# A hybrid decoder block: where the meta rows are loaded, how the first two tiles are normalized, and when the last 16 rows and V's second blocks are handled

## The chip, the cores and the metric

The kernel runs on one core of a Trainium2 chip. The metric is the device time of one execution in microseconds (us); several executions are timed, and one more is recorded by the hardware profiler. The engines are PE (TensorE, matrix products; PEld is its weight loads), DVE (VectorE), ACT (ScalarE), POOL (GpSimd) and SP (SyncE, which here only issues DMA transfers). ACTq and SPq are the instruction queues of ACT and SP where they issue transfers. Each engine takes its instructions in the order in which the program lists them.

## The reference

1,024 rows of `x` with 16 learned meta rows ahead of them (1,040 rows of 1,024 columns) are normalized, projected once into all branches, mixed by causal pooling and by attention with forget gates, merged and projected back.

```python
h = concat([meta, x])                               # 1040 x 1024
h = h * rsqrt(mean(h * h) + 1e-6) * norm_g
proj = h @ w_in                                     # u, z, q, k, v, z_attn, f, g_pool, g_attn
y_pool = (trailing_mean(u) - u) @ pool_w * pool_scale * silu(z_pool)
y_attn = forgetting_attention(q, k, v, log_sigmoid(f + b_forget)) * silu(z_attn)
merged = sigmoid(g_pool) * (y_pool @ w_up_pool) + sigmoid(g_attn) * (y_attn @ w_up_attn)
out = rmsnorm(x + merged @ w_out, final_norm_g)     # meta rows dropped
```

## The kernel before

Only the startup is touched, the first 60 us of some 743. It does three things.

**Normalizing.** The 1,040 rows are nine tiles `xts[0]` to `xts[8]`, eight of 128 rows and the last of 16. Tile 0 is filled by two transfers on SP's queue, 112 rows of `x` and the 16 meta rows (`norm_load`, L171). `norm_stat` (L182) squares a tile on ACT with a running sum (`ss`), which ACT reads out in an instruction of its own; `rstd_of` (L110) adds the epsilon on DVE (L113) and takes the power -0.5 on POOL (L114). `norm_scale` (L187) multiplies the tile in two halves of 512 columns on DVE by the row's `rstd` and by `gb`. `gb` holds `norm_g` in all 128 rows; two products on PE make it in PSUM from one row of ones and the loaded `norm_g` (L391), with `warm_up` products around them.

**Transposing.** `norm_t` (L192) transposes a scaled tile on PE into PSUM in two halves of four 128 x 128 blocks (`pt`, `pn`). ACT copies each half, rounded, to `hh` (L212), and DVE subtracts this from PSUM to get the rest, `hl` (L213). Only then is the PSUM buffer free. `pt` comes from a pool of two buffers, `pn` is a single one; tile 6 uses both `pt`, tile 7 `pn` and then the `pt` that tile 6's first half had, the 16-row tile the other `pt`.

**Projecting.** Weights are split in the same way into `whi` and `wlo` (L401, L406). For the first head pair, Q, K and V are computed for four pieces of the sequence (`todo`, twelve steps n = 0 to 11: q, k, v for 0:256, 256:512, 512:768, 768:1040). One piece is 24 products (L152): eight `hh,whi`, eight `hl,whi`, eight `hh,wlo`. Q's results are copied by ACT to `qa` and by DVE to `ql` (L241, L245), K's to `ka` (L263, L266), V's by ACT to `vt` (L270). `v_blocks` (L276) transposes two 128-row blocks of `vt` on PE, and ACT and DVE write `V` (L284, L285). The 16-row tile's transposes stand inside step n = 8, behind its eight `hh,whi` products.

The order of all this on every engine is the order of the code (a manual schedule), written in the loop over `todo`: behind step n it transposes a tile ahead, scales another, and now and then makes blocks of V.

Of the kernel before, what the change touches and what calls it, by code (L numbers as in the profile page):

```python
# [8 lines left out]
F32 = mybir.dt.float32  # L9
F32R = mybir.dt.float32r  # L10
AF = mybir.ActivationFunctionType
ALU = mybir.AluOpType
AX = mybir.AxisListType

D = 1024
NM = 16
# [4 lines left out]
EPS = 1e-6  # L21
# [22 lines left out]
def r32(ap):  # L44
    return ap.bitcast(F32)
# [7 lines left out]
def tile_hybrid_block(ctx, tc, x, meta, norm_g, w_in, b_forget, pool_w, pool_scale,  # L53
                      w_up_pool, w_up_attn, w_out, final_g, out):
    nc = tc.nc
# [14 lines left out]
    sm = ctx.enter_context(tc.tile_pool(name="sm", bufs=2))  # L70
# [4 lines left out]
    psG = G_.enter_context(tc.tile_pool(name="psG", bufs=1, space=PS))  # L75
# [4 lines left out]
    epsp = cst.tile([128, 1], F32, name="epsp")  # L80
# [29 lines left out]
    def rstd_of(ss):  # L110
        n = ss.shape[0]
        r = sm.tile([128, 1], F32, name="rstd", bufs=4)
        nc.vector.tensor_scalar(r[:n], ss, EPS, None, op0=ALU.add)  # L113
        nc.gpsimd.tensor_tensor(r[:n], r[:n], epsp[:n], op=ALU.pow)  # L114
        return r
# [45 lines left out]
    def run(g):  # L161
        for _ in g:
            pass
# [1 line left out]
    A = ExitStack()  # L165
    ap_ = A.enter_context(tc.tile_pool(name="ap", bufs=1))

    gb = psG.tile([128, 2, 512], F32, name="gb")
    junk = gp.tile([128, D], F32, name="junk", tag="g")

    def norm_load(i):  # L171
        c0 = i * 128
        n = min(128, L - c0)
        xt = ap_.tile([128, D], F32, name="xt", tag="s", bufs=6)
        if i == 0:
            nc.sync.dma_start(xt[NM:], x2[:128 - NM, :])
            nc.sync.dma_start(xt[:NM], meta)
        else:
            nc.sync.dma_start(xt[:n], x2[c0 - NM:c0 - NM + n, :])
        return xt  # L180

    def norm_stat(xt, n):  # L182
        ss = sm.tile([128, 1], F32, name="ss")
        nc.scalar.activation(junk[:n], xt[:n], AF.Square, scale=D ** -0.5, accum_out=ss[:n])
        return rstd_of(ss[:n])

    def norm_scale(xt, n, r):  # L187
        for j, (c0, c1) in enumerate(HALVES):
            nc.vector.scalar_tensor_tensor(xt[:n, c0:c1], xt[:n, c0:c1], r[:n], gb[:n, j],
                                           op0=ALU.mult, op1=ALU.mult)  # L190

    def norm_t(i0, xt, n):  # L192
        c0 = i0 * 128
        if n < 128:
            both = psT.tile([128, KO, n], F32, name="pt")
            for i in range(KO):
                nc.tensor.transpose(both[:, i, :], xt[:n, i * 128:(i + 1) * 128], ident[:n, :n])
            for j in range(2):
                h_ = hh4[j][:, :, c0:c0 + n]
                part = both[:, 4 * j:4 * j + 4]  # L200
                nc.scalar.activation(h_, part, AF.Copy)  # L201
                last = nc.vector.tensor_tensor(hl4[j][:, :, c0:c0 + n], part, r32(h_), op=ALU.subtract)
            return last
        for j in range(2):
            if (2 * i0 + j) % 3 == 2:
                pt = psG.tile([128, 4, 128], F32, name="pn")
            else:
                pt = psT.tile([128, 4, 128], F32, name="pt")
            for i in range(4):
                nc.tensor.transpose(pt[:, i, :n], xt[:n, (4 * j + i) * 128:(4 * j + i + 1) * 128], ident[:n, :n])  # L210
            h_ = hh4[j][:, :, c0:c0 + n]
            nc.scalar.activation(h_, pt[:, :, :n], AF.Copy)  # L212
            last = nc.vector.tensor_tensor(hl4[j][:, :, c0:c0 + n], pt[:, :, :n], r32(h_), op=ALU.subtract)  # L213
        return last
# [21 lines left out]
    def q_piece(p, w, t0, t1):  # L236
        c0, c1 = t0 - NM, t1 - NM
        ps = yield from g_proj(w, t0, t1)

        def hi(e, r):  # L240
            nc.scalar.activation(QA[p, e][r, c0:c1], ps[rows(e)[0]], AF.Copy, scale=0.125)  # L241

        def lo(e):
            a, _ = rows(e)
            nc.vector.scalar_tensor_tensor(QL[p, e][a, c0:c1], ps[a], 0.125, r32(QA[p, e][a, c0:c1]),  # L245
                                           op0=ALU.mult, op1=ALU.subtract)

        for group in EVAC[p > 0]:
            for e in group:
                hi(e, rows(e)[0])  # L250
                if not p:
                    hi(e, rows(e)[1])
            for e in group:
                lo(e)
                if p:
                    hi(e, rows(e)[1])

    def k_piece(p, w, t0, t1):
        ps = yield from g_proj(w, t0, t1)
        for group in EVAC[p > 0]:  # L260
            for e in group:
                a, o = rows(e)
                nc.scalar.activation(KA[p, e][a, t0:t1], ps[a], AF.Copy)  # L263
            for e in group:
                a, o = rows(e)
                nc.vector.tensor_tensor(KA[p, e][o, t0:t1], ps[a], r32(KA[p, e][a, t0:t1]), op=ALU.subtract)  # L266

    def v_piece(p, w, t0, t1):
        ps = yield from g_proj(w, t0, t1)
        nc.scalar.activation(VT[p][:, t0:t1], ps, AF.Copy)  # L270

    def v_alloc(p):
        for e in range(2):
            V[p, e] = ap_.tile([KB, NB, 2, 64], F32R, name="V", bufs=3)

    def v_blocks(p, b0, b1):  # L276
        pt = pj.tile([128, 4, 2, 64], F32, name="pj")
        for b in range(b0, b1):
            nc.tensor.transpose(pt[:, b - b0], VT[p][:, KS[b]:KS[b] + KB], ident)  # L279
            yield 109.0  # L280
        pv = pt[:, :b1 - b0]
        for e in range(2):
            vh = V[p, e][:, b0:b1, e, :]
            nc.scalar.activation(vh, pv[:, :, e, :], AF.Copy)  # L284
            nc.vector.tensor_tensor(V[p, e][:, b0:b1, 1 - e, :], pv[:, :, e, :], r32(vh), op=ALU.subtract)  # L285
# [91 lines left out]
    onesr = cst.tile([128, 128], F32R, name="onesr")  # L377
    nc.vector.memset(r32(onesr), 1.0)
    grow = ap_.tile([1, D], F32, name="grow", tag="t")
    nc.scalar.dma_start(grow, norm_g)  # L380
    nc.scalar.activation(junk[:1, :2], r32(onesr)[:1, :2], AF.Square)
    xts = {0: norm_load(0), 1: norm_load(1)}
    warm = psG.tile([128, 4, 128], F32, name="pn")

    def warm_up(n):
        for _ in range(n):
            nc.tensor.matmul(warm, onesr, onesr[:, None, :].to_broadcast([128, 4, 128]), start=True, stop=True)

    warm_up(WARM[0])
    for j, (c0, c1) in enumerate(HALVES):  # L390
        nc.tensor.matmul(gb[:, j], r32(onesr)[:1], grow[:, c0:c1], start=True, stop=True)  # L391
    warm_up(WARM[1])

    def load_raw(col, pool=None, tag="raw"):
# [4 lines left out]
    def split_hi(raw, pool, tag):  # L399
        hi = pool.tile([128, KO, 128], F32R, name="whi", tag=tag)  # L400
        nc.scalar.activation(hi, raw, AF.Copy)  # L401
        return hi

    def split_lo(raw, hi, pool, tag):
        lo = pool.tile([128, KO, 128], F32R, name="wlo", tag=tag)
        nc.gpsimd.tensor_tensor(lo, raw, r32(hi), op=ALU.subtract)  # L406
        return hi, lo
# [7 lines left out]
    def ntok(i):  # L415
        return min(128, L - 128 * i)

    alloc_k(0)
    for i in range(2):
        norm_scale(xts[i], 128, norm_stat(xts[i], 128))  # L420
    hq_ = split_hi(rq, wp, "wh")
    norm_t(0, xts[0], 128)
    wq = split_lo(rq, hq_, wp, "wl")
# [10 lines left out]
    for n, (kind, t0, t1) in enumerate(todo):  # L434
        if n + 4 < 9:
            xts[n + 4] = norm_load(n + 4)
        if kind == "q":
            run(q_piece(0, wq, max(NM, t0), t1))
        elif kind == "k":
            run(k_piece(0, wk, t0, t1))  # L440
        else:
            g = v_piece(0, wv, t0, t1)
            if n == 8:
                for _ in range(KO):
                    next(g)
                norm_t(8, xts[8], ntok(8))
            run(g)
        i = {0: 2, 1: 3, 3: 4, 4: 5, 6: 6, 7: 7}.get(n)
        if i is not None:
            norm_t(i, xts[i], ntok(i))  # L450
        if n == 0:
            hv_ = split_hi(rv, gp, "g")
            wv = split_lo(rv, hv_, gp, "g")
            VT[0] = gp.tile([128, L], F32, name="vt", tag="g")
            v_alloc(0)
        i = {1: 4, 2: 5, 4: 6, 5: 7, 6: 8}.get(n)
        if i is not None:
            norm_scale(xts[i], ntok(i), norm_stat(xts[i], ntok(i)))
        if n == 2:
            zero_q(0)  # L460
        if n == 4:
            wf = sm.tile([128, KO, H], F32, name="wf", bufs=1)
            nc.sync.dma_start(wf, w_in2[:, :, COL_F:COL_F + H])
        if n == 8:
            wfs = sm.tile([128, KO, 2 * H], F32R, name="wfs", bufs=1)
            nc.vector.tensor_copy(wfs[:, :, :H], wf)
            nc.vector.tensor_tensor(wfs[:, :, H:], wf, r32(wfs[:, :, :H]), op=ALU.subtract)
        if n in (4, 7, 10):
            run(v_blocks(0, 2 * (n // 3) - 2, 2 * (n // 3)))
    G_.close()  # L470
    psS = P_.enter_context(tc.tile_pool(name="psS", bufs=2, space=PS, reuse_waits="tile"))
    psO = P_.enter_context(tc.tile_pool(name="psO", bufs=1, space=PS, reuse_waits="tile"))
# [504 lines left out]
    for n, s in enumerate(steps):  # L977
# [10 lines left out]
        j, a = s  # L988
# [148 lines left out]
```

## Time and profile before

| what | value |
|---|---|
| median of 3 runs | 744.06 us (744.05 to 744.7) |
| the profiled execution | 744.31 us, its span on the core 742.6 us |
| PE busy | 731.9 us, 99% of the span |
| DVE, ACT, POOL busy | 528.8 us (71%), 376.8 us (51%), 305.1 us (41%) |
| the chain of work that ended last | 88% PE, 4% DVE, 1% ACT, 1% POOL |

The span runs from the first to the last instruction of the core. The chain is followed back from the last instruction, at each step to what released it. Where an engine is named in the chain, its work was what the end waited for.

### The profile page before, as it was taken

What the parts mean: (1) busy time and instruction counts of PE and PEld (TensorE: products, weight loads), DVE (VectorE), ACT (ScalarE), POOL (GpSimd) and SP (SyncE); (2) the same over time, 40 slices, a digit from 0 to 9 for tenths busy, and PEclk for the clock granted to TensorE, in tenths of its full rate; (3) what the DMA queues carried; (4) which work ended last, traced back from release to release, by engine and by line L of the source; (5) the groups of instructions that cost most, each with busy time, mean ns of one, the idle gap of its engine ahead of it and who ended that gap; (6) DMA issues with size and microseconds to landing.
All of it is one profiled execution on the core that took longest, in us unless ns stands there. A gap on an engine that the chain in (4) does not pass through costs nothing.

```text
span 742.6 us, 10618 instructions
## 1 busy us (share of the span) xinstructions
PE 731.9 (99%) x3686; PEld 623.9 (84%) x3686; DVE 528.8 (71%) x991; ACT 376.8 (51%) x736; POOL 305.1 (41%) x362
## 2 busy tenths in 40 slices
PE   8999999999999999999999999999999999999996
PEld 6997999988888898889988888888887888888885
DVE  5753577658769878788797687785298544887775
ACT  6662556456556545556563564452545322526445
POOL 4331235466426446346455383183358010006243
PEclk9999999999999999999999999999999999999999
DMA  9301122231352255312733255229376267672006
GB/s 310 79 10 48 29 86 83 62 100 20 97 160 62 83 103 124 100 53 55 191 81 87 80 147 138 72 88 309 94 195 216 82 199 266 214 257 71 1 0 227
DMA packets 82312, 86.89 MB, mean 117 GB/s; under 512 B 9889, under 2 KB 61089, under 8 KB 82226
## 3 DMA queue, kind: packets, MB, share of 16 engines
q1 hardware_dynamic: 78272, 77.29, 33.7%
q0 software_dynamic: 2112, 4.19, 3.6%
q10 hardware_dynamic: 1874, 4.72, 1.7%
q8 instruction: 29, 0.48, 0.3%
q14 instruction: 25, 0.20, 0.1%
HBM read 67.12 MB, written 27.46 MB: 127 GB/s over the span
## 4 chain that ended last, share of the span: by engine, by line
PE 88%; DVE 4%; POOL 1%; issue 1%; ACT 1%; POOLq 0%; ACTq 0%
PE pj L152 66%; PE pj L1017 8%; PE po L661 5%; PE ps L601 3%; PE ps L600 2%; PE pt L1017 2%; PE pj L486 1%; POOL yl L124 1%; DVE S L640 1%; DVE pl L645 0%; PE pj L279 0%; DVE ka L266 0%; DVE m L616 0%; DVE mx L625 0%; DVE pt L631 0%
## 5 line engine op out<-in xcount | busy, mean ns | idle before, releaser
L124 POOL TENSOR_TENSOR wlo<-raw,whi 128x256 fp32r<-128x256 f32 x148 | 121.2, 863 | 189.4 <-ACT whi L140 104.3
L152 PE MATMUL pj<-hh,whi 128*128 128x512 f32 (+4 forms) x768 | 179.2, 362 | 0.5 <-ACT hh L201 0.3
L152 PE MATMUL pj<-hl,whi 128*128 128x512 f32 (+4 forms) x768 | 177.1, 359 | 0.0
L152 PE MATMUL pj<-hh,wlo 128*128 128x512 f32 (+4 forms) x768 | 174.4, 358 | 0.0
L152 PEld LDWEIGHTS pj<-hh,whi 128*128 128x128 f32 x768 | 132.3, 190 | 18.5 <-ACT hh L201 0.5
L152 PEld LDWEIGHTS pj<-hh,wlo 128*128 128x128 f32 x768 | 132.3, 188 | 18.1
L152 PEld LDWEIGHTS pj<-hl,whi 128*128 128x128 f32 x768 | 131.7, 188 | 17.7
L645 DVE TENSOR_TENSOR pl<-S,ph 128x512 fp32r<-128x512 f32 (+4 forms) x112 | 85.8, 781 | 16.7 <-ACT ph L644 16.1
L653 POOL TENSOR_TENSOR acc<-acc,S 128x272 f32<-128x272 f32 (+4 forms) x80 | 76.4, 955 | 9.8 <-ACT S L641 3.7
L609 ACT ACTIVATE S<-ps,negc 128x400 f32<-128x400 f32 (+2 forms) x96 | 49.2, 514 | 46.1 <-DVE S L607 37.3
L641 ACT ACTIVATE S<-S 128x512 f32<-128x512 f32 (+4 forms) x112 | 49.5, 478 | 33.1 <-DVE S L640 32.9
L616 DVE TENSOR_TENSOR m<-m,S 128x272 f32<-128x272 f32 (+4 forms) x80 | 41.2, 515 | 24.1 <-ACT S L609 22.4
L644 ACT ACTIVATE ph<-S 128x512 fp32r<-128x512 f32 (+4 forms) x112 | 52.1, 480 | 11.8 <-PE po L661 10.7
L140 ACT ACTIVATE whi<-raw 128x1024 fp32r<-128x1024 f32 x37 | 39.1, 1057 | 31.9 <-PE pj L152 27.5
L640 DVE TENSOR_TENSOR S<-S,pt 128x512 f32<-128x512 f32 (+4 forms) x112 | 51.9, 498 | 0.8
L865 DVE TENSOR_TENSOR rl<-pj,rl 128x512 f32<-128x512 f32 x32 | 22.1, 690 | 33.7 <-PE pj L152 33.7
L607 DVE SCALAR_TENSOR_TENSOR S<-ps,negc,mask 128x128 f32<-128x128 f32 (+2 forms) x72 | 23.6, 329 | 21.1 <-PE ps L601 20.9
L317 ACT ACTIVATE st<-pj 128x512 f32<-128x512 f32 x40 | 23.7, 593 | 28.5 <-PE pj L152 19.0
L661 PE MATMUL po<-pl,V 128*128 128x512 f32 (+4 forms) x112 | 37.6, 336 | 0.1
L601 PE MATMUL ps<-ql,ka 128*128 128x512 f32 (+4 forms) x112 | 37.5, 334 | 0.0
L600 PE MATMUL ps<-qa,ka 128*128 128x512 f32 (+4 forms) x112 | 35.9, 321 | 0.5 <-ACT S L609 0.5
L1017 PE MATMUL pj<-opy 128*128 128x512 f32 (+1 forms) x168 | 36.3, 375 | 0.0
(187 smaller groups left out, 1105.5 us busy)
## 6 DMA issues: line engine op xcount, KB each, us to landing
raw<-in_w_in_dram SPq DMA_DIRECT2D x40, 512.0 KB, 3.9
sp_gp<-st SPq DMA_DIRECT2D x16, 256.0 KB, 2.1
td<-in_w_out_dram POOLq DMA_DIRECT2D x4, 1024.0 KB, 10.1
sp_ga<-st SPq DMA_DIRECT2D x16, 256.0 KB, 2.0
rl<-sp_gp SPq DMA_DIRECT2D x8, 512.0 KB, 5.0
rl<-sp_ga SPq DMA_DIRECT2D x8, 512.0 KB, 4.8
W<-td SPq DMA_DIRECT2D x8, 512.0 KB, 5.2
xr<-in_x_dram SPq DMA_DIRECT2D x8, 512.0 KB, 4.0
```

The lines of the kernel that those rows point to most:

```text
L124: ins = nc.gpsimd.tensor_tensor(out[:, c:c + 256], x[:, c:c + 256], y[:, c:c + 256], op=op)
L152: nc.tensor.matmul(ps, a, b, start=(i == 0), stop=(i == len(seq) - 1))
L600: nc.tensor.matmul(ps[:kb, c0:], ka[:, k0:k0 + kb], qa[:, q0 + c0:q0 + 512], start=True, stop=False)
L601: nc.tensor.matmul(ps[:kb, c0:], ka[:, k0:k0 + kb], ql[:, q0 + c0:q0 + 512], start=False, stop=True)
L609: nc.scalar.activation(s[:kb, f0:], ps[:kb, f0:], AF.Identity, bias=nb_)
L640: nc.vector.tensor_tensor(s[:kb, c0:], s[:kb, c0:], self.pm[:kb, c0:], op=ALU.subtract)
L641: exps.append(nc.scalar.activation(s[:kb, c0:], s[:kb, c0:], AF.Exp))
L644: nc.scalar.activation(ph[:kb, c0:], s[:kb, c0:], AF.Copy)
L645: dves.append(nc.vector.tensor_tensor(pl[:kb, c0:], s[:kb, c0:], r32(ph[:kb, c0:]), op=ALU.subtract))
L653: accs.append(nc.gpsimd.tensor_tensor(acc[:kb, c0:], acc[:kb, c0:], s[:kb, c0:], op=ALU.add))
L661: nc.tensor.matmul(self.po[:, c0:], v, r[:kb, c0:], start=(b == 0 and i == 0), stop=(b == self.nb - 1 and i == 1))
L1017: nc.tensor.matmul(ps, pick(A_, k, p)[:, i * 128:(i + 1) * 128], pick(B_, k, q)[:, c0:c1], start=start and n == 0, stop=n == 11, skip_grou ...
```

## The change

Four edits, all in the startup.

1. The meta rows of tile 0 are loaded from ACT's queue instead of SP's. In the code this stands behind `norm_g`'s load and a small activation that brings in ACT's function table.
2. `gb` becomes two tiles of 512 columns, one for each product, so that a scaling waits for its own half.
3. For tiles 0 and 1, `norm_stat2` squares the first 512 columns on ACT and the other 512 on DVE, each with a sum of its own; the two sums and the epsilon are added by one DVE instruction.
4. Tile 8 (16 rows) is squared and scaled right behind tile 7 (step n = 5 instead of n = 6), and V's blocks 2 and 3 are made behind step n = 8 instead of n = 7.

```diff
-    gb = psG.tile([128, 2, 512], F32, name="gb")
+    gb = [psG.tile([128, 512], F32, name=f"gb{j}") for j in range(2)]
...
-            nc.sync.dma_start(xt[:NM], meta)
+            nc.scalar.dma_start(xt[:NM], meta)
...
+    def norm_stat2(xt, n):
+        ss = [sm.tile([128, 1], F32, name="ss") for _ in range(2)]
+        nc.scalar.activation(junk[:n, :512], xt[:n, :512], AF.Square, scale=D ** -0.5, accum_out=ss[0][:n])
+        nc.vector.scalar_tensor_tensor(junk[:n, 512:], xt[:n, 512:], 1.0 / D, xt[:n, 512:], op0=ALU.mult, op1=ALU.mult,
+                                       accum_out=ss[1][:n])
+        r = sm.tile([128, 1], F32, name="rstd", bufs=4)
+        nc.vector.tensor_scalar(r[:n], ss[0][:n], ss[1][:n], EPS, op0=ALU.add, op1=ALU.add)
+        nc.gpsimd.tensor_tensor(r[:n], r[:n], epsp[:n], op=ALU.pow)
+        return r
...
-            nc.vector.scalar_tensor_tensor(xt[:n, c0:c1], xt[:n, c0:c1], r[:n], gb[:n, j],
+            nc.vector.scalar_tensor_tensor(xt[:n, c0:c1], xt[:n, c0:c1], r[:n], gb[j][:n],
...
-        nc.tensor.matmul(gb[:, j], r32(onesr)[:1], grow[:, c0:c1], start=True, stop=True)
+        nc.tensor.matmul(gb[j], r32(onesr)[:1], grow[:, c0:c1], start=True, stop=True)
...
-        norm_scale(xts[i], 128, norm_stat(xts[i], 128))
+        norm_scale(xts[i], 128, norm_stat2(xts[i], 128))
...
-        i = {1: 4, 2: 5, 4: 6, 5: 7, 6: 8}.get(n)
-        if i is not None:
+        for i in {1: (4,), 2: (5,), 4: (6,), 5: (7, 8)}.get(n, ()):
             norm_scale(xts[i], ntok(i), norm_stat(xts[i], ntok(i)))
...
-        if n in (4, 7, 10):
-            run(v_blocks(0, 2 * (n // 3) - 2, 2 * (n // 3)))
+        if n in (4, 8, 10):
+            run(v_blocks(0, *{4: (0, 2), 8: (2, 4), 10: (4, 6)}[n]))
```

The order of instructions on DVE around steps n = 5 to 7, before. `xt_364` is tile 7, `xt_411` tile 8, `pt_536` and `pt_543` the two transposed halves of tile 6, `pj_505` the result of step 6 (Q) and `pj_557` that of step 7 (K):

```order
L113 TENSOR_SCALAR rstd_500<-ss_498 128x1
L189 SCALAR_TENSOR_TENSOR xt_364<-xt_364,rstd_500,gb_119 128x512 x2
L245 SCALAR_TENSOR_TENSOR ql_218<-pj_505,qa_217 64x256
L245 SCALAR_TENSOR_TENSOR ql_220<-pj_505,qa_219 64x256
L213 TENSOR_TENSOR hl0_114<-pt_536,hh0_112 128x4x128
L213 TENSOR_TENSOR hl1_115<-pt_543,hh1_113 128x4x128
L113 TENSOR_SCALAR rstd_552<-ss_550 16x1
L189 SCALAR_TENSOR_TENSOR xt_411<-xt_411,rstd_552,gb_119 16x512 x2
L266 TENSOR_TENSOR ka_151<-pj_557,ka_151 64x256
```

The same place on DVE in the change, where tile 7 is `xt_369`, tile 8 `xt_416` and tile 6's halves are `pt_548` and `pt_555`:

```order
L113 TENSOR_SCALAR rstd_505<-ss_503 128x1
L199 SCALAR_TENSOR_TENSOR xt_369<-xt_369,rstd_505,gb0_119 128x512
L199 SCALAR_TENSOR_TENSOR xt_369<-xt_369,rstd_505,gb1_120 128x512
L113 TENSOR_SCALAR rstd_512<-ss_510 16x1
L199 SCALAR_TENSOR_TENSOR xt_416<-xt_416,rstd_512,gb0_119 16x512
L199 SCALAR_TENSOR_TENSOR xt_416<-xt_416,rstd_512,gb1_120 16x512
L255 SCALAR_TENSOR_TENSOR ql_223<-pj_517,qa_222 64x256
L255 SCALAR_TENSOR_TENSOR ql_225<-pj_517,qa_224 64x256
L223 TENSOR_TENSOR hl0_114<-pt_548,hh0_112 128x4x128
L223 TENSOR_TENSOR hl1_115<-pt_555,hh1_113 128x4x128
L276 TENSOR_TENSOR ka_152<-pj_562,ka_152 64x256
```

The sum and the scaling of tile 8 have moved ahead of the two `ql` and of the two `hl` of tile 6.

The first instructions on ACT in the change, where `xt_129` is tile 0 and `xt_132` tile 1:

```order
L390 DMA grow_126<-in_norm_g_dram 1x1024
L391 ACT_TABLE_LOAD
L391 ACTIVATE junk_121<-onesr_124 1x2
L177 DMA xt_129<-in_meta_tokens_dram 16x1024
L189 ACTIVATE junk_121,ss_154<-xt_129 128x512
L189 ACTIVATE junk_121,ss_163<-xt_132 128x512
```

The issue of the meta rows now stands behind the table load and the small activation, and the two squares are of 512 columns.

The first work on DVE in the change, behind the constants:

```order
L190 SCALAR_TENSOR_TENSOR junk_121,ss_155<-xt_129 128x512
L193 TENSOR_SCALAR rstd_158<-ss_154,ss_155 128x1
L199 SCALAR_TENSOR_TENSOR xt_129<-xt_129,rstd_158,gb0_119 128x512
L199 SCALAR_TENSOR_TENSOR xt_129<-xt_129,rstd_158,gb1_120 128x512
L190 SCALAR_TENSOR_TENSOR junk_121,ss_164<-xt_132 128x512
L193 TENSOR_SCALAR rstd_167<-ss_163,ss_164 128x1
L199 SCALAR_TENSOR_TENSOR xt_132<-xt_132,rstd_167,gb0_119 128x512
```

DVE now squares half of tile 0 ahead of its sum, and half of tile 1 between tile 0's second scaling and tile 1's sum.

## Rows read from the trace of the kernel before

**Rows 1.** Busy time on the page: us, share of the span, instructions.

```profile
PE 731.9 (99%) x3686; PEld 623.9 (84%) x3686; DVE 528.8 (71%) x991; ACT 376.8 (51%) x736; POOL 305.1 (41%) x362
```

**Rows 2.** The chain of waits, 0 to 60 us: start, us, what.

```profile
45.21 1.29 DVE hl L213 x2
```

**Rows 3.** Timeline, 40.5 to 47.5 us: start, us, engine, line, operation, [idle before <-releaser].

```profile
41.66 0.42 PEld L210 LDWEIGHTS pt<-ident,xt 128*128 128x128 f32 x4 [0.22 <-DVE hl L213]
...
43.71 0.32 PEld L197 LDWEIGHTS pt<-ident,xt 16*128 16x128 f32 x4 [0.43 <-issue]
43.74 0.39 PE L197 MATMUL pt<-ident,xt 16*128 16x16 f32 x4 [0.26 <-issue]
...
44.35 0.32 PEld L197 LDWEIGHTS pt<-ident,xt 16*128 16x128 f32 x4 [0.32 <-DVE xt L189]
44.35 0.42 PE L197 MATMUL pt<-ident,xt 16*128 16x16 f32 x4 [0.22 <-DVE xt L189]
...
47.18 0.42 PEld L152 LDWEIGHTS pj<-hh,whi 128*128 128x128 f32 x3 [0.55 <-ACT hh L201]
47.18 0.52 PE L152 MATMUL pj<-hh,whi 128*128 128x272 f32 x2 [0.34 <-ACT hh L201]
```

**Rows 4.** Timeline of DVE, 31 to 50 us.

```profile
37.89 0.15 DVE L113 TENSOR_SCALAR rstd<-ss 128x1 f32<-128x1 f32 x1 [1.02 <-ACT junk L184]
...
40.03 0.85 DVE L245 SCALAR_TENSOR_TENSOR ql<-pj,qa 64x256 fp32r<-64x256 f32 x2
40.91 1.29 DVE L213 TENSOR_TENSOR hl<-pt,hh 128x512 fp32r<-128x512 f32 x2
42.12 0.13 DVE L113 TENSOR_SCALAR rstd<-ss 16x1 f32<-16x1 f32 x1
42.90 1.40 DVE L189 SCALAR_TENSOR_TENSOR xt<-xt,rstd,gb 16x512 f32<-16x512 f32 x2 [0.65 <-POOL rstd L114]
```

**Rows 5.** Timelines of the head, 0 to 16 us, all engines.

```profile
1.25 0.42 SPq L177 DMA_DIRECT2D xt<-in_meta_tokens_dram  x1
...
1.38 1.28 ACT L381 ACT_TABLE_LOAD   x1 [1.38 <-PEq L1123]
...
2.68 0.20 ACT L381 ACTIVATE junk<-onesr 1x2 f32<-1x2 f32 x1
...
5.11 1.06 ACT L184 ACTIVATE junk<-xt 128x1024 f32<-128x1024 f32 x1 [2.23 <-DMA xt<-in_meta_tokens_dram]
5.20 1.91 PE L391 MATMUL gb<-grow,onesr 1*128 1x512 f32 x2
6.07 0.19 ACT L184 ACTIVATION_READ_ACCUMULATOR junk<-xt 128x1 f32 x1
...
7.20 1.41 DVE L189 SCALAR_TENSOR_TENSOR xt<-xt,rstd,gb 128x512 f32<-128x512 f32 x2 [0.75 <-PE gb L391]
...
8.52 0.15 DVE L113 TENSOR_SCALAR rstd<-ss 128x1 f32<-128x1 f32 x1
...
9.34 1.41 DVE L189 SCALAR_TENSOR_TENSOR xt<-xt,rstd,gb 128x512 f32<-128x512 f32 x2 [0.68 <-POOL rstd L114]
...
11.40 0.71 PEld L210 LDWEIGHTS pt<-ident,xt 128*128 128x128 f32 x4 [0.53 <-DVE hl L213]
...
12.17 2.11 PE L152 MATMUL pj<-hh,whi 128*128 128x240 f32 x8
...
14.12 1.07 PE L152 MATMUL pj<-hl,whi 128*128 128x240 f32 x8
```

**Rows 6.** DMA issues of the whole run: transfer, issuing queue, count, KB each, us to landing.

```profile
out_dram<-o ACTq DMA_DIRECT2D x8, 256.0 KB, 2.8
...
xt<-in_meta_tokens_dram SPq DMA_DIRECT2D x1, 64.0 KB, 3.7
```

**Rows 7.** Timeline of ACT and its queue, 646 to 649 us.

```profile
647.40 0.34 ACTq L1003 DMA_DIRECT2D fgb<-in_final_norm_g_dram  x1
647.93 1.04 ACT L855 ACTIVATE rl<-rl 128x1024 f32<-128x1024 f32 x1
```

**Rows 8.** Clock granted to PE, in tenths, 40 slices of the span.

```profile
PEclk9999999999999999999999999999999999999999
```

## Prediction

> **What bounds the kernel now.** I read the page first: TensorE (PE) is busy 99% of the span [rows 1], so a change outside it pays only where PE is seen waiting. Then the chain of waits over the first 60 us. It leaves PE in one stretch of the startup, where it runs over VectorE (DVE) [rows 2], so I read the timeline there. Every engine's queue is in order here. Call the nine 128-row pieces of the input tile 0 to tile 8 (tile 8 has the last 16 rows).
>
> In the stretch from 41 to 47 us the reader is to see two kinds of wait on PE [rows 3]. The second half of tile 7's transposes started at 41.66, after 0.22 us of waiting for DVE's `hl`: it writes the PSUM buffer that tile 6's first half held, which DVE's first `hl` of tile 6 (started 40.91) frees. Then the 16-row transposes waited for DVE's scaling of tile 8, and the next projection at 47.18 waited for ScalarE's (ACT's) copy of those 16 rows. On DVE [rows 4] the order is: sum and scaling of tile 7 (37.89), two `ql` (40.03), two `hl` of tile 6 (40.91), and only then tile 8 (42.12 and 42.90).
>
> In the head [rows 5] the first matrix product needs tile 1, not only tile 0, and tile 1 passes through DVE last. DVE scaled tile 0 from 7.20, released by PE's `gb` product, whose last pass ends at 5.20 + 1.91 = 7.11. It took tile 1's sum at 8.52 and scaled it from 9.34. Behind that scaling DVE frees a PSUM buffer, for which tile 1's last transposes waited until 11.40, and the first product follows at 12.17.
>
> **The change, part by part.**
>
> *16 rows scaled sooner, middle stretch.* The order listing shows tile 8's sum and scaling moved ahead of the two `ql` and of tile 6's `hl` on DVE. They bring their own wait along: from 42.12 (sum) to 42.90 is 0.78 us, in which GpSimd (POOL) takes the power and DVE stands idle, and the scaling takes 1.40 for 16 rows, in slots of 1.42. So 2.20 us are put in at 40.03. ACT's square and read for tile 8 also move ahead. Taken at a whole tile's 0.96 to the read and 0.19 for it [rows 5], behind tile 7's read, which ended at about 37.86 (DVE's wait for it ended at 37.89), they end near 39.0, before DVE is free at 40.03. ACT's copies of tile 6 come about 1 us later for it, still before DVE, 2.2 us later itself, wants them. So tile 6's first `hl` starts at 40.91 + 2.20 = 43.11, and tile 7's second transposes at 41.66 + 2.20 = 43.86: that wait had no slack, since PE already stood there.
>
> What PE does from those transposes to the product at 47.18 took 5.52 us. Waits in it: on the weight-load track 0.43 + 0.32 + 0.55 = 1.30, on the matmul track 0.26 + 0.22 + 0.34 = 0.82 [rows 3]. With tile 8 ready early and DVE clear of it, these waits go: 4.22 or 4.70 us of work remain. The product would start between 43.86 + 4.22 = 48.08 and 43.86 + 4.70 = 48.56: **0.90 to 1.38 us later** than now. I take 1.05, nearer the load track, because matmul ends are modelled. Tile 8's copy is no longer waited for at 48: its transposes, which now begin 2.1 us behind tile 7's (43.74 against 41.66), come near 46.
>
> *V's second blocks later.* Two transposes, two ACT copies and two DVE subtracts go from before the projection to behind it. PE's two transposes stay inside the 5.52 us, so nothing is added. ACT no longer stands at V's second copy with tile 8's behind it; that is part of the 0.34 already counted. The PSUM buffer that they take is now the one that `ql` frees (near 43.1 in the new order), long before 48. Cost zero; without that cover, at most the 0.34.
>
> *Squares on two engines (tiles 0 and 1).* ACT's 1,024-column square becomes a 512-column one on ACT and another on DVE. The 1,024-column one starts its read 0.96 us behind its own start, and the read takes 0.19; I take 0.54 and 0.19 for half the columns, an estimate that leaves a tenth of a microsecond fixed. Two scalings of 512 columns on DVE take 1.41, in slots of about 0.67, 0.74 for one [rows 5]. Call s the time at which both squares of tile 0 start (5.11 on ACT now). Its sum then starts at about s + 0.75, and its scaling 0.82 behind that (8.52 to 9.34 for tile 1 now): the first half at s + 1.57, the second at s + 2.24.
>
> *`gb` in two tiles.* The first half can then be scaled before the second product ends. The second half cannot: 7.20, as now. Here DVE's order decides: scaling of the second half (7.20), **tile 1's square on DVE (7.87)**, its sum (about 8.64, behind the square's 0.74 and a hand-over of 0.03), scaling of tile 1 at 9.46, against 9.34. The gain on tile 0 is given back by the new DVE instruction: +0.12 us at the least. A DVE operation with an accumulated sum does not occur in the trace; its extra cost is between nothing and ACT's 0.19 for a read. I take half, **+0.2**. The Trainium skill (VectorE: DVE Perf Modes, section Two Vector instructions with no wait between them) counts such an operation as two instructions, the main one and an accumulator read; by that the upper end, +0.3, would hold. No run here shows it yet.
>
> *Meta rows on ScalarE's queue.* In ACT's order the issue stands behind the table load and the small activation. Now it is issued on SyncE's queue at 1.25 and lands 3.7 us later [rows 6], and ACT's first square starts at 5.11 for it. How early ACT's queue can issue it isn't shown directly. Nearest: the load of `fgb`, which stands behind an activation, was issued at 647.40, before that activation ran at 647.93 [rows 7]. If a table load is likewise only queued, the issue comes at about 1.4, where the table load itself started (1.38). By the 3.7 us it then lands at 5.1 and s is 5.25; by less than that, s is earlier, since those 3.7 us hold the wait behind the x rows that were issued just ahead on the same queue. Then s + 2.24 is 7.49 at most, and with any s up to 4.96 it is 7.20 that binds. I take 7.20. The following loads on SyncE's queue go out 0.42 earlier; nothing on the path waits for them.
>
> *Sum.* +0.2 in the head and +1.05 in the middle: +1.25 us. Behind 47 us the chain is almost all PE in one fixed order, with no later slack that I found, so the shift stays. On the profiled execution (744.31, itself 0.25 above the median) it gives 745.6; on the median 744.06 + 1.25 = **745.3 us**, 0.17% more. About 0.2% (1.5 us) is what a measurement of this kernel can tell from no change, so this counts as no change, on the slow side. Its own range, from the bounds (head 0.1 to 0.6, middle 0.9 to 1.4), is 745.0 to 746.0.
>
> **Rivals.**
>
> *The meta rows come late (slower).* If ACT's queue stands until the table load ends, the issue comes at 2.66 instead of 1.25. Landing is then between 2.8 us later (the stores on ACT's queue, the quickest rows of that queue) and 3.7 [rows 6]: s is 5.6 to 6.5, the second half of tile 0 starts at s + 2.24, 7.85 to 8.75, and the head costs 0.85 to 1.75 instead of 0.2. With the middle that is 1.9 to 2.8 us: 746.0 to 746.9, middle 746.4. It decides (slower by over 1.5 us) once s passes about 5.2. For it: the table load stands ahead in the order. Against it speaks [rows 7].
>
> *The queue stands longer still.* The small activation ran at 2.68, 0.02 behind the end of the load's 1.28 us [rows 5], so nothing followed the load. If as much again followed it for the queue, the issue would come at about 4.0, s at 6.9 to 7.8, and the time would be near 747.7. The Trainium skill (ScalarE: Activation LUTs, section What ACT_TABLE_LOAD costs) gives 1,283 ns plus a drain of about 1,380 ns for every switch; the load agrees, the drain isn't in the trace.
>
> *DVE has room after all (faster).* If tile 8's block fits ahead of tile 6's `hl` without pushing it, PE's waits vanish and nothing is lost: -1.30 - 0.22 (the wait at 41.66) + 0.2 in the head, so about 742.7. It needs DVE free 2.2 us before 40.03; against it, tile 7's sum waited for ACT until 37.89 [rows 4], and nothing in the change makes that ACT work earlier.
>
> *PE's clock comes up at another moment.* The granted clock reads full in every slice of the span [rows 8], but the first product's eight matmuls took 1.95 us (12.17 to 14.12) and the next eight 1.07 [rows 5]: PE ran at the lower of its two levels (1.2 of 2.4 GHz) until 14. Before that it was busy with transposes; the new order spreads them differently. Coming up before the first pass gives back about 0.9 (744.4), one pass later costs as much (746.2).
>
> **How the numbers follow.** Forecast 0.53, meta late 0.20, queue longer 0.02, DVE room 0.15, clock 0.10. The range takes in the late rival up to 746.5, its middle, and of the fast one the half above 742.9, where I set the lower end. Faster by over 0.2% means below 742.57: half of the DVE-room case, 0.08. Slower means above 745.55: a quarter of the forecast's cases (0.13), nearly all of the late ones (0.20), half of the clock's (0.05): 0.38. The rest, 0.54, is no change.
>
> **What would show it.** Right: tile 8's scaling on DVE ahead of `ql`; PE idle some 2.2 us ahead of tile 7's second transposes, on DVE's `hl`; no PE wait at the 16-row transposes or for their copy; tile 0's first half scaled well before 7.1 and tile 1's scaling not earlier than 9.4. The meta issue near 1.4 or near 2.7 settles the first rival. Wrong: tile 7's transposes starting within 1 us of now, or tile 1 scaled before 9.2.

## The result, and the profile after

The change made the kernel slower: median **747.23 us** of 6 runs (746.32 to 749.27) against 744.09 us of 6 runs of the kernel before, ratio 1.0045 (95% interval 1.0034 to 1.0055). The forecast of 745.3 us and its range, up to 746.5, were passed. The profiled execution of the changed kernel took 746.49 us, its span 744.8: 2.18 and 2.2 us over those of before.

Line numbers of the changed kernel are 10 higher than those quoted of before from the new function on (L189 is now L199, L213 is L223), and 9 higher behind the loop over `todo`. First the page: busy time, and the chain that ended last. PE's busy time is what it was [rows 1]; the span has grown around it.

```profile
span 744.8 us, 10623 instructions
...
PE 731.7 (98%) x3686; PEld 624.3 (84%) x3686; DVE 531.1 (71%) x995; ACT 376.7 (51%) x736; POOL 305.2 (41%) x362
...
PE 89%; DVE 4%; issue 1%; ACT 0%; POOLq 0%; POOL 0%; ACTq 0%
```

The view of waits on PE shows where (engine, line, what was waited for: total us, times, longest). The first, third and fourth have no equal of that size before.

```profile
PE pt L220 <- DVE hl L223: 2.1, 1, 2.1
PE pn L397 <- DVE car L529: 1.3, 1, 1.3
PE pt L220 <- DVE xt L199: 1.2, 1, 1.2
PE pn L220 <- issue: 1.1, 1, 1.1
```

The head, from the timeline of the changed kernel over 0 to 18 us (start, duration, engine, line, operation, idle time before it and its releaser); it answers to [rows 5].

```profile
1.25 0.42 SPq L179 DMA_DIRECT2D xt<-in_x_dram  x1
...
1.38 1.28 ACT L391 ACT_TABLE_LOAD   x1 [1.38 <-PEq L1132]
1.44 0.34 ACTq L177 DMA_DIRECT2D xt<-in_meta_tokens_dram  x1
...
6.58 0.69 DVE L190 SCALAR_TENSOR_TENSOR junk<-xt 128x512 f32<-128x512 f32 x1 [5.29 <-DMA xt<-in_meta_tokens_dram]
6.58 0.63 ACT L189 ACTIVATE junk<-xt 128x512 f32<-128x512 f32 x1 [3.71 <-DMA xt<-in_meta_tokens_dram]
...
7.19 0.08 DVE L190 DVE_READ_ACCUMULATOR junk<-xt 128x1 f32 x1
7.38 0.21 DVE L193 TENSOR_SCALAR rstd<-ss 128x1 f32<-128x1 f32 x1
...
8.27 1.41 DVE L199 SCALAR_TENSOR_TENSOR xt<-xt,rstd,gb 128x512 f32<-128x512 f32 x2 [0.67 <-POOL rstd L194]
...
11.29 1.41 DVE L199 SCALAR_TENSOR_TENSOR xt<-xt,rstd,gb 128x512 f32<-128x512 f32 x2 [0.68 <-POOL rstd L194]
...
14.12 2.24 PE L152 MATMUL pj<-hh,whi 128*128 128x240 f32 x8
...
16.16 1.64 PE L152 MATMUL pj<-hl,whi 128*128 128x240 f32 x8
```

And the issue of the meta rows on the page, with the time to landing, which answers to [rows 6]:

```profile
xt<-in_meta_tokens_dram ACTq DMA_DIRECT2D x1, 64.0 KB, 5.0
```

The issue on ACT's queue went out at 1.44, 0.06 behind the start of the table load: it did not wait for that load. But the rows took 5.0 us to land instead of 3.7, though issued only 0.19 us later. Both squares of tile 0 waited for them until 6.58 (s, in the prediction's word; 5.11 before). Tile 1 is scaled at 11.29 instead of 9.34, the first product starts at 14.12 instead of 12.17: **+1.95 us in the head**.

The middle, from the timeline over 39 to 50.2 us, answers to [rows 3, 4]:

```profile
40.66 1.41 DVE L199 SCALAR_TENSOR_TENSOR xt<-xt,rstd,gb 128x512 f32<-128x512 f32 x2 [0.66 <-POOL rstd L114]
...
41.98 0.13 DVE L113 TENSOR_SCALAR rstd<-ss 16x1 f32<-16x1 f32 x1
...
42.77 1.39 DVE L199 SCALAR_TENSOR_TENSOR xt<-xt,rstd,gb 16x512 f32<-16x512 f32 x2 [0.65 <-POOL rstd L114]
...
44.09 0.84 DVE L255 SCALAR_TENSOR_TENSOR ql<-pj,qa 64x256 fp32r<-64x256 f32 x2
...
44.97 1.29 DVE L223 TENSOR_TENSOR hl<-pt,hh 128x512 fp32r<-128x512 f32 x2
...
45.72 0.66 PE L220 MATMUL pt<-ident,xt 128*128 128x128 f32 x4 [2.10 <-DVE hl L223]
...
47.26 0.66 PE L207 MATMUL pt<-ident,xt 16*128 16x16 f32 x8
...
49.97 0.50 PE L152 MATMUL pj<-hh,whi 128*128 128x272 f32 x2
```

DVE scales tile 8 ahead of `ql` and of tile 6's `hl`, and PE stands 2.10 us ahead of tile 7's second transposes. The later waits of [rows 3] are gone. The projection that began at 47.18 begins at 49.97, 2.79 later; 1.95 of that is the head's, so the **middle costs 0.84**. The two make 2.79, the spans differ by 2.2: before's profile holds a wait of 0.49 on POOL's `yl` at 570 us that after's does not. (It stands in one more of the profiles below, e9's, with 0.54, and in none of the others here; what sets it was not looked into.)

The median lies 3.14 over before's, more than these 2.79. The six runs show why: four had a mean granted clock of 0.997 or 0.998 and took 746.32 to 747.42, two had 0.992 and 0.993 and took 748.63 and 749.27.

### The profile page after: what moved, and what is told of

Same layout as the page of the kernel before. It is cut to its first block, busy times and chain, and to the rows that moved or that the text cites. A ratio compares the mean times of both kernels' runs of the same rounds, so it can differ in the third digit from the quotient of the medians.

```text
span 744.8 us, 10623 instructions
## 1 busy us (share of the span) xinstructions
PE 731.7 (98%) x3686; PEld 624.3 (84%) x3686; DVE 531.1 (71%) x995; ACT 376.7 (51%) x736; POOL 305.2 (41%) x362
## 4 chain that ended last, share of the span: by engine, by line
PE 89%; DVE 4%; issue 1%; ACT 0%; POOLq 0%; POOL 0%; ACTq 0%
PE pj L152 67%; PE pj L1026 8%; PE po L670 5%; PE ps L610 3%; PE ps L609 2%; PE pt L1026 2%; PE pj L495 1%; DVE S L649 1%; PE pj L289 0%; DVE pl L654 0%; DVE ql L255 0%; DVE m L625 0%; DVE mx L634 0%; DVE ka L276 0%; DVE pt L640 0%
```

## The experiments

My account was that two separate losses add up: the late landing of the meta rows, because their transfer shares the DMA engines with tile 1's 512 KB, and tile 8's block ahead of tile 6's `hl`. One rival puts the landing down to ACT's queue itself; another puts a part of the time down to PE's clock. Where an expectation says A it is this account, and B a rival of it.

Each run was timed beside runs of the kernel before, and its ratio is against those: their median was 744.27 us for e1 to e4, 744.55 us for e5 and e7 to e9, and 744.22 us for e6 and e10. These three groups ran on three different chips. What a timeline shows is from one execution of each kernel.

### One part at a time

**e1, the whole change but with the meta rows on SP's queue.**

```diff
-            nc.scalar.dma_start(xt[:NM], meta)
+            nc.sync.dma_start(xt[:NM], meta)
```

Expected: 

> The whole change, but the meta rows are loaded on SyncE's queue again. Theory A (two separate losses: the meta rows land late from ScalarE's queue, and tile 8 in front of tile 6's subtraction on VectorE holds up TensorE): the squares of tile 0 start near 5.1 us instead of 6.6, tile 1 is scaled at about 9.8, 0.5 us later than in the kernel before (one accumulating instruction more on VectorE), the wait of 2.1 us at tile 7's transposes stays; about 745.1 us, some 2 us below the change. Theory B (most of the loss is TensorE's clock, which drops or comes up late because TensorE idles 2.1 us in the middle): the time stays above 746 and the mean granted clock of some runs below 0.995.

Measured: 745.3 us (744.87 to 748.54, 12 runs), ratio 1.0027 (1.0016 to 1.0039). In its profile the rows landed in 4.1 us, s is 5.46, the first product 13.01; PE's wait at tile 7 is 2.09. So between these two profiles 1.11 of the head's 1.95 goes with the queue, and the middle's loss stays. The landing on SP's queue is itself not always the same: over the eight profiles that have the rows there it lies between 3.3 and 4.1 us, and this is the latest of them. The runs stand in two groups: eight of 744.87 to 745.49 at a clock of 0.997 to 0.999, four of 748.05 to 748.54 at 0.992 to 0.994.

**e2, before with the meta rows on ACT's queue and nothing else** (the same line, the other way).

Expected: 

> The kernel before, with the meta rows on ScalarE's queue alone. Theory A: the issue comes at about 1.44 us, the rows land near 6.4, the first square starts near 6.6 instead of 5.1, and everything behind shifts by 1.5 us: about 745.5 us. Theory B: the transfer costs the 1.5 us, but without the 2.1 us wait in the middle the clock stays as it was, no run far above the others. If the late landing belongs to the earlier start of the other loads in the change alone, it would show here too, since the SyncE queue is the same.

Measured: 745.37 us (744.46 to 746.03, 11 runs), ratio 1.0012 (1.0003 to 1.002). ACT's first square starts at 6.77, the first product at 13.74 (+1.57 in that profile), and the landing takes 5.2 us (DMA view over 0 to 12 us):

```profile
xt<-in_meta_tokens_dram ACTq DMA_DIRECT2D x1, 64.0 KB, 5.2
```

The queue alone brings most of the head's loss. Four runs lie at 744.46 to 744.49, near before's. It may be that the rows came less late in those, but only the profiled execution shows its landing.

**e3, before with tile 8 scaled sooner and nothing else.**

```diff
-        i = {1: 4, 2: 5, 4: 6, 5: 7, 6: 8}.get(n)
-        if i is not None:
+        for i in {1: (4,), 2: (5,), 4: (6,), 5: (7, 8)}.get(n, ()):
```

Expected: 

> The kernel before, with tile 8 (16 rows) scaled right behind tile 7 and nothing else changed; V's second blocks stay where they were. Theory A: TensorE waits about 2.1 us for tile 6's subtraction at tile 7's second transposes; the waits at the 16-row transposes and for their copy shrink; about +0.9 us, 745.0 us. Theory B: the same waits, and in some runs a lower mean granted clock with 1 to 3 us more. A rival, that the move is good and only the other edits cost: below 744.0.

Measured: 745.45 us (744.72 to 748.48, 11 runs), ratio 1.0024 (1.0012 to 1.0036), and again two groups: six runs of 744.72 to 745.45 at 0.997 or 0.998, five of 747.64 to 748.48 at 0.992 to 0.995. The profiled execution, 747.96 us, belongs to the upper one and shows what is different there. Its windows (stretch: length, busy time of each engine, granted clock, DMA share, GB/s):

```profile
41.50:44.20 2.70, 0.61 (x7) 0.37 (x5) 2.65 (x6) 1.75 (x5) 0.00 (x0) 1.00 0.00 0
44.20:46.00 1.80, 1.80 (x14) 1.77 (x14) 1.72 (x4) 0.77 (x2) 0.00 (x0) 0.88 0.00 0
46.00:48.00 2.00, 2.00 (x14) 1.76 (x13) 1.57 (x5) 0.45 (x3) 0.00 (x0) 0.50 0.00 0
48.00:50.00 2.00, 2.00 (x11) 2.00 (x11) 0.55 (x3) 0.17 (x1) 0.00 (x0) 0.50 0.00 0
50.00:52.00 2.00, 2.00 (x11) 2.00 (x11) 0.00 (x0) 0.38 (x1) 0.00 (x0) 0.50 0.00 0
...
52.50:56.00 3.50, 3.50 (x30) 3.50 (x29) 0.00 (x0) 2.22 (x5) 1.12 (x2) 1.00 0.02 5
```

And the timeline of its PE:

```profile
41.51 0.60 PE L210 MATMUL pn<-ident,xt 128*128 128x128 f32 x4
44.20 0.66 PE L210 MATMUL pt<-ident,xt 128*128 128x128 f32 x4 [2.09 <-DVE hl L213]
...
44.83 1.44 PE L152 MATMUL pj<-hh,whi 128*128 128x256 f32 x8
...
47.16 2.08 PE L152 MATMUL pj<-hl,whi 128*128 128x256 f32 x8
49.03 1.91 PE L152 MATMUL pj<-hh,wlo 128*128 128x256 f32 x8
50.74 1.92 PE L152 MATMUL pj<-hh,whi 128*128 128x272 f32 x8
52.50 1.16 PE L152 MATMUL pj<-hl,whi 128*128 128x272 f32 x8
```

Behind the wait of 2.09 us the granted clock falls from 1.00 to 0.50, from 2.4 to 1.2 GHz, and is back by 52.5. By the share of 0.88 in the stretch to 46.00 it fell near 45.6, so PE ran at the lower level for nearly 7 us. From tile 7's second transposes to the pass at 52.50 it takes 8.30 us. The same work in e1's profile, where the granted clock stayed at 1.00 from 40 to 56 us:

```profile
44.69 0.66 PE L220 MATMUL pt<-ident,xt 128*128 128x128 f32 x4 [2.09 <-DVE hl L223]
...
50.03 1.17 PE L152 MATMUL pj<-hl,whi 128*128 128x272 f32 x8
```

It took 5.34 us there. The difference, 2.96, is about the distance between the two groups of e3, whose medians are 744.99 and 747.96. This was not in the prediction.

**e4, before with V's second blocks later and nothing else.**

```diff
-        if n in (4, 7, 10):
-            run(v_blocks(0, 2 * (n // 3) - 2, 2 * (n // 3)))
+        if n in (4, 8, 10):
+            run(v_blocks(0, *{4: (0, 2), 8: (2, 4), 10: (4, 6)}[n]))
```

Expected: 

> The kernel before, with V's second blocks behind step 8 and nothing else changed. Theory A: ScalarE's copy of the 16 rows no longer stands behind V's second copy, so TensorE's wait of 0.34 us ahead of step 9 goes: about 743.7 us. A rival, that the blocks' own copies now delay the next steps: 744.1 or more. Theory B says the same as A.

Measured: 743.75 us (742.92 to 744.35, 11 runs), ratio 0.9991 (0.9982 to 0.9999). The wait of 0.34 for ACT's copy is gone, the projection starts at 46.97 in spite of a head 0.12 later than before's. The two waits at tile 8's transposes stay, 0.48 and 0.22. This part is a small gain.

**e5, edits 2 and 3 alone** (`gb` in two tiles, squares on two engines; queue, tile 8 and V as before).

Expected: 

> The kernel before, with the squares of tiles 0 and 1 on two engines and norm_g's product in two tiles, nothing else. Theory A (VectorE's order decides: its square of tile 1 stands behind the scaling of tile 0, which cannot end before norm_g's second product): tile 1 is scaled near 9.5 to 10.2 us instead of 9.34, the first product starts 0.2 to 0.9 us later, about 744.7 us; no run above 746, since no wait of 2 us arises. A rival, that earlier work on tile 0 helps: 743.9 or less.

Measured: 744.47 us (744.02 to 744.89, 11 runs), ratio 0.9998 (0.9989 to 1.0007): nothing. Its timeline of the head says why:

```profile
4.78 0.63 ACT L189 ACTIVATE junk<-xt 128x512 f32<-128x512 f32 x1 [1.92 <-DMA xt<-in_meta_tokens_dram]
...
6.48 1.41 DVE L199 SCALAR_TENSOR_TENSOR xt<-xt,rstd,gb 128x512 f32<-128x512 f32 x2 [0.67 <-POOL rstd L194]
7.81 0.68 DVE L190 SCALAR_TENSOR_TENSOR junk<-xt 128x512 f32<-128x512 f32 x1
8.42 0.08 DVE L190 DVE_READ_ACCUMULATOR junk<-xt 128x1 f32 x1
8.61 0.21 DVE L193 TENSOR_SCALAR rstd<-ss 128x1 f32<-128x1 f32 x1
...
9.50 1.41 DVE L199 SCALAR_TENSOR_TENSOR xt<-xt,rstd,gb 128x512 f32<-128x512 f32 x2 [0.68 <-POOL rstd L194]
```

Here the rows landed in 3.4 us and tile 0 was scaled 0.72 us sooner than before, yet tile 1 0.16 later: DVE's square of tile 1, its read and the longer sum stand between. Tile 1's scaling starts 4.72 us behind s; in e1 it is 5.46 to 10.18, also 4.72, and after 6.58 to 11.29, 4.71. So with the split squares every tenth of a microsecond in the landing goes through to the first product.

### Why the meta rows land late

**e8, before with the meta rows on ACT's queue, but issued ahead of `norm_g`.**

```diff
-            nc.sync.dma_start(xt[:NM], meta)
+            nc.scalar.dma_start(xt[:NM], meta)
...
+    xts = {0: norm_load(0)}
     nc.scalar.dma_start(grow, norm_g)
     nc.scalar.activation(junk[:1, :2], r32(onesr)[:1, :2], AF.Square)
-    xts = {0: norm_load(0), 1: norm_load(1)}
+    xts[1] = norm_load(1)
```

Expected: 

> The kernel before, with the meta rows on ScalarE's queue but issued ahead of norm_g, at 0.80 us instead of 1.44. If the late landing (5.0 us from the issue) comes from sharing the DMA engines with tile 1's load, which was issued at 1.25 us ahead of it: the rows land within about 3.5 us, the first square starts near 4.5 to 5.0, norm_g arrives some 0.4 us later and its second product ends near 7.5; about 744.2 us. If a transfer on ScalarE's queue is slow in itself: again 5 us from the issue, landing near 5.8, 744.8 us or more.

Measured: 746.0 us (744.92 to 746.66, 11 runs), ratio 1.0019 (1.001 to 1.0028). Issued at 0.80, ahead of tile 1's load at 1.25, the rows land in 3.3 us:

```profile
xt<-in_meta_tokens_dram ACTq DMA_DIRECT2D x1, 64.0 KB, 3.3
```

The time expected, 744.2 us, was missed, because now `norm_g` comes late. It was issued at 1.26, behind the meta rows on ACT's queue and 0.01 us behind tile 1's load on SP's; from the timelines of PE and DVE:

```profile
4.92 3.78 PE L392 MATMUL gb<-grow,onesr 1*128 1x512 f32 x4 [1.52 <-DMA grow<-in_norm_g_dram]
...
8.79 1.41 DVE L189 SCALAR_TENSOR_TENSOR xt<-xt,rstd,gb 128x512 f32<-128x512 f32 x2 [2.52 <-PE gb L392]
```

**e9, e2 with tile 1's load, and with it all later loads on SP's queue, held until the meta rows have landed** (one run).

```diff
-            nc.sync.dma_start(xt[:NM], meta)
+            mload.append(nc.scalar.dma_start(xt[:NM], meta))
...
-            nc.sync.dma_start(xt[:n], x2[c0 - NM:c0 - NM + n, :])
+            ld = nc.sync.dma_start(xt[:n], x2[c0 - NM:c0 - NM + n, :])
+            if i == 1:
+                behind(ld, mload[0])
...
-    nc.sync.dma_start(psc, pool_scale[0].rearrange("(g c) -> c g", c=128))
+    last_ld = nc.sync.dma_start(psc, pool_scale[0].rearrange("(g c) -> c g", c=128))
...
-    nc.sync.dma_start(pw, pool_w[0].rearrange("g c d -> c g d"))
+    after(nc.sync.dma_start(pw, pool_w[0].rearrange("g c d -> c g d")), last_ld)
```

The last two edits put a later load in its place behind another.

Expected: 

> The kernel before, with the meta rows on ScalarE's queue behind norm_g, and tile 1's load (with all loads behind it on SyncE's queue) held until the meta rows have landed. The time is of no interest; the landing is. Sharing with tile 1's load: issued at 1.44, landed within 3.0 us, near 4.4. Slow in itself: again 5 us.

Measured: 746.15 us in one run; the time pays for the held load, and the landing is what counts. From the DMA view over 0 to 12 us:

```profile
xt<-in_meta_tokens_dram ACTq DMA_DIRECT2D x1, 64.0 KB, 3.7
```

With the same issue (1.43) on the same queue, and tile 1's load not sent until 5.17, the rows landed in 3.7 us instead of 5.2. So ACT's queue is not slow in itself, and the table load does not hold the transfer. The run expected 3.0 us, and the rows took 3.7 with no later load beside them. By itself e9 does not tell tile 1's load from the weight loads that it held as well. But in e8 and in before those loads went out as usual, and the rows, issued ahead of tile 1's load, landed in 3.3 and 3.7 us. What is left is the place in time: behind tile 1's load 5.0 and 5.2 us, ahead of it or without it 3.3 to 4.1. `norm_g` in e8 is in line with this but no proof, since it stood behind the meta rows on its own queue too. The Trainium skill (DMA: Bandwidth & Descriptors, section Issuing engines are not separate DMA queues) says that transfers started from several engines run on the same 16 DMA engines and interleave; these runs are in line with it, 5.2 us behind the other load and 3.7 with that load held.

### Whether the wait brings the clock down

**e7, e3 with 16 more products of 256 columns on PE ahead of tile 7's second transposes.** They write a buffer of their own and add nothing to the result.

```diff
+            if i0 == 7 and j == 1:
+                fil = pj.tile([128, 512], F32, name="pj")
+                for f in range(16):
+                    nc.tensor.matmul(fil[:, :256], wq[0][:, f % KO, :], hh[f % KO][:, :256], start=True, stop=True)
```

Expected: 

> The kernel before with tile 8 scaled sooner (as in the run of that edit alone, where 5 of 11 executions lay near 748 and 6 near 745), and 16 more matrix products of 256 columns, whose result nothing uses, put on TensorE ahead of tile 7's second transposes, where it waited 2.1 us. Theory B2 (the slow executions come from TensorE's clock falling to its lower level behind that wait): the wait is filled, no execution lies above 746 and the mean granted clock stays at 0.997 or more; about 745.0 us in all. If the clock falls for another reason, the two groups stay.

Measured: 746.27 us (745.67 to 747.71, 11 runs), ratio 1.0023 (1.0014 to 1.0032). All eleven runs have a granted clock of 0.997 or more; of e3's eleven, five had 0.995 or less. By the clock the upper group of e3 is gone. By the time the expectation failed: six of the eleven lie above 746. Each against its own runs of before, the median is 1.72 up here and e3's lower group (744.99) 0.72, so the level is 1.0 over that group. The timeline of PE shows most of the reason:

```profile
41.92 2.12 PE L208 MATMUL pj<-hh,whi 128*128 128x256 f32 x16
...
44.24 0.65 PE L214 MATMUL pt<-ident,xt 128*128 128x128 f32 x4 [0.20 <-DVE hl L217]
...
45.80 1.18 PE L152 MATMUL pj<-hh,whi 128*128 128x256 f32 x8 [0.69 <-DVE ka L270]
```

The added products take a buffer of `pj`, so the next projection waits 0.69 for DVE to empty another. The filler is no remedy, but it separates the two things: the same lateness of tile 7 (44.24, e3 44.20) without PE standing still, and the clock does not fall. Two limits remain. e3 and e7 ran on different chips, and no kernel with the wait left open ran beside e7. And e7 does not tell the wait from the whole stretch without a product: in e3 PE began nothing but transposes from 41.51 until 44.83.

Over all runs: where PE stood 2.1 us here (after, e1, e3), 11 of 29 executions had a clock of 0.995 or less. Where it did not (e2, e4, e5, e6, e7, e8, e10), none of 77 had. The chip is not what divides them: of the runs of e1 to e4, all on one chip, 9 of 23 fell with the wait (e1, e3) and none of 22 without it (e2, e4).

### The good parts together

**e6, `gb` in two tiles, squares on two engines for tile 0 only, V's blocks later; queue and tile 8 as before.**

```diff
-            nc.scalar.dma_start(xt[:NM], meta)
+            nc.sync.dma_start(xt[:NM], meta)
...
-        norm_scale(xts[i], 128, norm_stat2(xts[i], 128))
+        norm_scale(xts[i], 128, norm_stat2(xts[i], 128) if i == 0 else norm_stat(xts[i], 128))
...
-        for i in {1: (4,), 2: (5,), 4: (6,), 5: (7, 8)}.get(n, ()):
+        i = {1: 4, 2: 5, 4: 6, 5: 7, 6: 8}.get(n)
+        if i is not None:
```

The lines are against the changed kernel.

Expected: 

> A version meant to keep what helped: meta rows on SyncE's queue, norm_g in two tiles, the squares on two engines for tile 0 alone (tile 1's square whole on ScalarE, so that VectorE does not get one between the two scalings), tile 8 where it was, V's second blocks later. Theory A: tile 1 is scaled near 8.7 to 9.0 us instead of 9.34 (-0.4 to -0.6), and the wait for the 16 rows' copy goes (-0.34): about 743.3 us. If the head gains nothing: 743.75, as with V's blocks alone.

Measured: 743.74 us (743.48 to 744.84, 11 runs), ratio 0.9994 (0.9985 to 1.0003). Tile 1 is scaled at 9.63, not near 8.7 to 9.0 as expected: without DVE's square its sum waits for ACT, whose square of tile 1 waited here for that tile's own load until 7.62 (6.53 in before's profile).

**e10, e6 with tile 8's square and sum at n = 5 and its scaling at n = 6.**

```diff
-        i = {1: 4, 2: 5, 4: 6, 5: 7, 6: 8}.get(n)
+        i = {1: 4, 2: 5, 4: 6, 5: 7}.get(n)
...
+        if n == 5:
+            r8 = norm_stat(xts[8], ntok(8))
+        if n == 6:
+            norm_scale(xts[8], ntok(8), r8)
```

Expected: 

> The same, and tile 8's square and sum right behind tile 7's, but its scaling left behind tile 6's subtraction on VectorE. Theory A: VectorE no longer idles 0.65 us for the power ahead of tile 8's scaling, TensorE's transposes of the 16 rows wait about 0.7 us less, and tile 7's transposes wait only some 0.1 us more: about 742.8 us. No execution above 745, since no wait of 2 us arises.

Measured: 743.73 us (742.98 to 744.54, 11 runs), ratio 0.9992 (0.9983 to 1.0001). The waits at tile 8's transposes are gone, and 0.47 has come back at tile 7's `hl`: about the same loss, one place earlier, where 0.1 was expected. By their ratios neither beats e4 (0.9991), which is V's edit alone.

## Why the prediction was wrong

**The head, the step that failed: "I take 7.20".** That tile 0's second half would wait for `gb` held only for s up to 4.96, which needs the rows to land within about 3.4 us of an issue at 1.4; at the 3.7 us of [rows 6] the prediction's own sum gave 7.49. I argued that 3.7 was an upper end, since it held a wait behind the x rows on SP's queue. No run shows that wait: on ACT's queue, with the later loads held, the rows took 3.7 us as well (e9). In the change they stood behind tile 1's load instead and took 5.0. The head cost 1.95, not 0.2 nor the 0.6 that I set as its upper bound. The rest of that chain was sound: with the measured s of 6.58 its own sum gives 6.58 + 2.24 = 8.82, 1.62 behind 7.20, and with the 0.2 a cost of 1.82.

The part of +0.2 was itself sized well. The DVE square of tile 1 delays its scaling (e5: 9.50 against 9.34). The accumulator's read is an instruction of its own, 0.08 us; the Trainium skill (VectorE: DVE Perf Modes, section Two Vector instructions with no wait between them) counts two, and the trace agrees. The sum with two operands took 0.21 where the old one took 0.15.

**The first rival had the result and the wrong cause.** Late meta rows were priced at s up to 6.5 and 0.85 to 1.75 us, measured 6.58 and 1.95. Its cause, a queue that stands behind the table load, did not happen: [rows 7] was the right row for it, and the issue went out at 1.44 as read from there. The prediction tied late rows to a late issue and had no case of a timely issue that lands late.

**The middle was right in its mechanism, and a little too large.** Tile 8 ahead of `ql`, PE's wait on `hl` (2.10) and the waits that go were as forecast. The block put in on DVE was 2.11 us instead of 2.20, and PE took 4.25 us from tile 7's second transposes (45.72) to the projection (49.97), inside the 4.22 to 4.70. So the sum, +1.05 in a range of 0.90 to 1.38, measured 0.84, just under the range. PE no longer waits at the 16-row transposes or for their copy, as predicted.

**V's blocks** at cost zero: e4 shows the cover of 0.34 named for them, and a gain about that size.

**The missing term: the clock.** The clock rival looked only at the rise in the first 16 us. What it looked at did happen in part, and cost nothing: the second pass took 1.64 us in the change instead of 1.07, so the third began 2.60 later than before (17.63 against 15.03), but from there to the next projection PE took 2.39 us in before, waits included, and 1.74 in the change, so that one is 1.95 late again (19.37 against 17.42). That a wait of 2.2 us, which the prediction itself put into PE's path, could bring the clock down was not asked. It cost 2.96 us in e3's profiled execution. In the changed kernel two of six runs have the lower mean clock, and they lift the median from 746.77 (the other four) to 747.23. Without them the median would still lie above the range, by the head.

What stays open: why the clock fell behind that wait in 11 executions of 29 and not in the others. After's own profile has the wait of 2.10 and a granted clock of 1.00 behind it. Also open is whether the wait itself or the whole stretch of transposes around it brings the clock down, and how long the meta rows took in executions that were not profiled.

## What to carry to other kernels

A small load that starts the critical path belongs ahead, in time of issue, of the big loads that are needed after it, whichever queue it is on; here another queue did not take it out of such a load's way. When a change makes PE stand still in one piece, price the clock behind it as well as the wait, and look at several executions, since only some may show it. Before an instruction moves ahead on an engine that PE waits for, count its whole block, idle hand-over included, against the slack of what it passes.

## What the hardware showed that I had not expected

- 64 KB issued 0.19 us behind a load of 512 KB on another queue took 5.0 and 5.2 us to land (after, e2); with that load held back 3.7 (e9), issued ahead of it 3.3 (e8).
- With a wait of 2.1 us on PE, 11 of 29 executions had a mean granted clock of 0.995 or less. In the one of them that was profiled it fell to half behind the wait, for nearly 7 us, at a price of 2.96 us.
- A transfer queued on ACT behind a table load of 1.28 us was issued 0.06 us after that load began.
